# Expert weights fetched two parts to a transfer, fourteen small places, and the ranks of the experts made ahead of the first expert

## The chip, the cores and the metric

The kernel runs on one core of one Trainium2 chip. The metric is device time in microseconds. Several runs of the kernel before agree within 2.4 us, so about 0.2% is what a measurement of this kernel can tell from no change.

## The reference, cut to what matters

Two transformer blocks over 512 tokens of 1024 features, all in float32. The change lies in the second block's mixture of experts: 32 experts, 4 per token, each expert three 1024x1024 matrices (403 MB in all).

```python
def moe(xn, w_router, b_router, w_gate, b_gate, w_up, b_up, w_down, b_down):
    logits = (xt @ w_router).astype(jnp.float32) + b_router
    top_vals, top_idx = lax.top_k(logits, TOP_K)          # 4 of 32
    gates = jax.nn.softmax(top_vals, axis=-1)
    ...
        gt = jnp.minimum(xb @ w_gate[e] + b_gate[e], 7.0)
        up = jnp.clip(xb @ w_up[e] + b_up[e], -7.0, 7.0)
        hdn = (up + 1.0) * (gt * jax.nn.sigmoid(1.702 * gt))
        return hdn @ w_down[e] + b_down[e]
    ...
    out = jnp.zeros((N, D)).at[st].add(ybuf[dest] * sg[:, None])
```

## The kernel before, in words

**Float32 products** are made of two float32r halves: a weight tile `wraw` is cast to `whi` on ACT and the rest `wlo` is taken on DVE (`split`, L292); a product is three matmuls, hi·hi, hi·lo and lo·hi (`mm3`, L321 to L323).

**The expert stage** goes through `seq`: for each place p the 8 parts (128 rows of 1024) of gate, the 8 of up, and then the 8 of down of place p-1; 24 parts to a place, 768 in all. Places, not experts: a table `RANK` says which rank (by number of tokens) each place takes. Most places are big, with 112 rows (`CAP`): 6 matmuls of 512 columns to a part. The places in `FEW` are small, with 64 rows: there x_hi and x_lo stand side by side in one 128-wide operand, so that 4 matmuls do a part (L1684 to L1688); ahead of the next step ACT copies the lower half to `lower` and two matmuls fold it in (`hop`, `save_lower`, `fold_lower`). `FEW` has 12 places before. Tokens of an expert beyond its place's rows would go to a loop behind the stage (`overflow_rows`).

**Order of the work.** `fetch(i + 6)` ahead of part i splits parts 5 ahead of the product (`SPLIT_AHEAD`); `put(i, f)` hangs other work on part i (table `beside`), and `in_order` holds every engine but SP to the order in which the code is written. SP issues each weight transfer as soon as a buffer is free and the last transfer on the same of eight completion semaphores has landed. Raw tiles, `whi` and `wlo` share one ring of 4 KB slots that `Plan` hands out: 14 `s` slots, `x0`, `x1`, 15 `e` and 6 `y` slots.

**The start of the stage.** `choose`, `position` and `one_hot` find the tokens of expert 0; `gather(0)` fetches its rows on POOL's queue (L1494); `scale_rows` scales them, `turn_rows(0)` turns them on PE (L1654) and `split_rows(0)` splits them (`he`). Experts 0 and 1 have places 0 and 1 whatever their counts. From place 2 on a place needs the ranks: `ranks` (L1806, L1810) compares the 32 keys, `matches`, `places` and `places_end` (L1833 to L1849) make the row of each token's entry and scatter 16 tables, `picks` and `order_product` make `ranked`, which SP reads (`values_load`, L1528) ahead of the first weights of place 2. `third_place` (L1815 to L1822) finds the tokens of place 2. Before, all of it hangs on parts 0 to 13. The 16 tables come back on ACT's queue at parts 24 to 27 (`table_slots`, L1719), and `sum_tables` and `all_slots` make the slots of all other places of them.

Of the kernel before, what the change touches and what calls it, by code (L numbers as in the profile page):

```python
# [21 lines left out]
P = 128  # L22
# [12 lines left out]
FEW = [p for p in range(2, 30) if (p * 5) % 14 < 5] + [30, 31]  # L35
RANK = {p: p for p in (0, 1)}
RANK.update({p: 2 + i for i, p in enumerate(FEW)})
RANK.update({p: 2 + len(FEW) + i for i, p in enumerate(q for q in range(2, NE) if q not in FEW)})
# [26 lines left out]
def host_layout(i):  # L65
# [60 lines left out]
class Plan:  # L126
# [7 lines left out]
    def __init__(self, stages, slots, ahead, added=None, until=None, early=0):  # L134
# [8 lines left out]
        class State:  # L143
# [16 lines left out]
            def load(st):  # L160
                st.loads += 1
                return st.take(st.loads - 1)

            def split(st):
                i = st.splits
                ok = (st.loads > i or st.load()) and (kinds[i] == "r" or (st.take(i) and st.take(i)))
                if ok:
                    st.free.append(st.got[i][0])
                    st.splits += 1
                return ok  # L170

            def begin(st, u):

                i, k = first[u + 1], ahead(u)
                while i < n and k:
                    k -= kinds[i] == "p"
# [58 lines left out]
def build(tc, I, out, dbg=None, stop=None):  # L235
# [3 lines left out]
    with es:  # L239
# [558 lines left out]
        def attention(g, fill):  # L798
# [7 lines left out]
            for i in range(len(units) + AHEAD):  # L806
# [4 lines left out]
                if i in fill:  # L811
# [19 lines left out]
        open_ring("ring2", stages + ["p"] * (NE * 24), lambda u: 2 if u < experts - 1 else SPLIT_AHEAD if u >= experts else 0,  # L831
                  {forward - 1: [f"g{i}" for i in range(3)], mixer - 1: [f"p{i}" for i in range(5)], experts - 1: ['x0', 'e14', 'e13', 'e12', 'x1', 'e3', 'e4', 'e7', 'e8', 'e9', 'e10', 'e11', 'e5', 'e6', 'e0', 'e1', 'e2'], experts: ['y0', 'y1', 'y2', 'y3', 'y4', 'y5']}, {"g": mixer - 1, "p": mixer + 3}, mixer)
# [485 lines left out]
        for e in range(2):  # L1318
            nc.vector.tensor_scalar(out=keys[:, e:e + 1], in0=keys[:, e:e + 1], scalar1=100000.0 * (e - 2), scalar2=None, op0=ALU.add)
# [137 lines left out]
        more = [f"e{i}" for i in range(15)]  # L1457
# [5 lines left out]
        pick0 = early.tile([P, 2, 2], F32R, name="pick0")  # L1463
# [12 lines left out]
        for q in range(2):  # L1476
            nc.vector.tensor_copy(pick0[64 * q:64 * q + 64, q], eye[64 * q:64 * q + 64, 0:2])
# [44 lines left out]
        parts, expert = [], {0: 0, 1: 1}  # L1522

        def weights_of(n, p, k):
            rows = slice(k * P, (k + 1) * P)
            if p not in expert:
# [3 lines left out]
            return I["we_" + n][p, rows] if p < 2 else I["we_" + n][expert[p], rows, :].rearrange("o p n -> (o p) n")  # L1530
# [52 lines left out]
        weigh(1)  # L1583
        choose(0)
        position(0)
        one_hot(slot_of[:, :, 0:1], (0,), oh0)
        slot_products(ptok, oh0, (0,), 4, told)
        gi0 = tokens_of(ptok, 0)
# [5 lines left out]
        for tt in (1, 0):  # L1594
            store_normed(tt)
        weigh(0)
        pn = W["rb"][:, 2 * NT]
        for t2 in range(NT):
            nc.tensor.matmul(pn, ones, chosen[:, t2], start=t2 == 0, stop=t2 == NT - 1)
# [3 lines left out]
        nc.vector.scalar_tensor_tensor(out=keys, in0=pn, scalar=float(NE), in1=keys, op0=ALU.mult, op1=ALU.add)  # L1603
        nc.vector.tensor_copy(room, pn)
# [87 lines left out]
        def biased_product(ps, a, p, j):  # L1692

            def bias_of(start):
                t, r = (pick0, p) if p < 2 else (pick, RANK[p])
# [44 lines left out]
        psum, rows, pts = {}, {}, {}  # L1740
# [62 lines left out]

        def ranks():
            t = row_tile("cmp").rearrange("p (e f) -> p e f", f=NE)
            nc.vector.tensor_tensor(out=t, in0=keys[:, None, :].to_broadcast([P, NE, NE]), in1=keys[:, :, None].to_broadcast([P, NE, NE]), op=ALU.is_lt)  # L1806
            rows["cmp"] = t

        def ranks_end():
            nc.vector.reduce_sum(rank, rows.pop("cmp"), axis=AX)  # L1810

        def third_place():

            t = small.tile([P, NE], F32, tag="third", name="third", bufs=1)
            nc.vector.tensor_scalar(out=t, in0=rank, scalar1=float(RANK[2]), scalar2=None, op0=ALU.is_equal)  # L1815
            col = early.tile([P, NT, 1], F32, name="col2")
            u = row_tile("sel")[:, :NT * NE].rearrange("p (t e) -> p t e", e=NE)
            nc.vector.scalar_tensor_tensor(out=u, in0=slot_of, scalar=1.0, in1=t[:, None, :].to_broadcast([P, NT, NE]), op0=ALU.add, op1=ALU.mult)
            nc.vector.reduce_sum(col.rearrange("p t o -> p (t o)"), u, axis=AX)
            nc.vector.tensor_scalar(out=col, in0=col, scalar1=-1.0, scalar2=None, op0=ALU.add)  # L1820
            rows["oh2"] = new_one_hot()
            one_hot(col, range(NT), rows["oh2"])  # L1822

        def third_products():
            pts["tok2"] = ps_tr()
            slot_products(pts["tok2"], rows.pop("oh2"), range(NT), 2, [])

        def third_tokens():
            rows["gi2"] = tokens_of(pts.pop("tok2"), 2)

        def matches():
            t = rows["eq"] = row_tile("eqs")
            nc.vector.tensor_tensor(out=t[:, 0:512].rearrange("p (t k e) -> p t k e", k=4, e=NE), in0=iota[:, None, None, 0:NE].to_broadcast([P, NT, 4, NE]),  # L1833
                                    in1=choice[:, :, :, None].to_broadcast([P, NT, 4, NE]), op=ALU.is_equal)
            both = rows["both"] = row_tile("both")[:, :NT * NE].rearrange("p (t e) -> p t e", e=NE)
            nc.vector.scalar_tensor_tensor(out=both, in0=slot_of, scalar=float(NE), in1=rank[:, None, :].to_broadcast([P, NT, NE]), op0=ALU.mult, op1=ALU.add)

        def places():
            t = rows["eq"]
            v = [t[:, 512 * q:512 * q + 512].rearrange("p (t k e) -> p t k e", k=4, e=NE) for q in range(2)]  # L1840
            nc.vector.tensor_tensor(out=v[1], in0=v[0], in1=rows.pop("both")[:, :, None, :].to_broadcast([P, NT, 4, NE]), op=ALU.mult)

        def places_end():
            t = rows["eq"]
            at_ = small.tile([P, NT * 4], F32, tag="at", name="at", bufs=1)
            nc.vector.reduce_sum(at_, t[:, 512:D].rearrange("p (n e) -> p n e", e=NE), axis=AX)
            nc.vector.tensor_copy(place.rearrange("p t k -> p (t k)"), at_)
            for j, tb in enumerate(tables):
# [371 lines left out]
```

## Time and profile before

| | us |
|---|---|
| median of 3 runs | 2107.16 (2106.08 to 2108.41) |
| the profiled execution, its own time | 2103.72 |
| its span, first to last instruction | 2102.0 |
| PE busy | 1997.9 (95%) |
| DVE busy | 1647.1 (78%) |
| ACT busy | 1375.3 (65%) |
| weights of the experts | 768 transfers of 512 KB |

PE is TensorE's matmuls, DVE is VectorE, ACT ScalarE, POOL GpSimd, SP SyncE; ACTq and SPq are the queues on which these engines issue transfers. The granted clock is a share of TensorE's full 2.4 GHz. A matmul's record runs into the next one's, so sums of records are more than the time they cover; busy time counts each moment once.

### The profile page before, as it was taken

To read this page: it belongs to the slowest core of one execution; us is meant where nothing else is said; L and a number is where in the kernel's file an instruction comes from. 1 tells how busy PE (TensorE), PEld (TensorE's weight loads), DVE (VectorE), ACT (ScalarE), POOL (GpSimd) and SP (SyncE) were. 2 spreads that over 40 slices of the span, in tenths; PEclk is the share of its full clock that TensorE was granted. 3 is DMA by queue.
4 is the path that set the end of the run, shared out by engine and by line. 5 is a ranking of instruction groups with operands and counts; after the bars stand their busy time and mean duration, and the time that the engine had idled before them with its cause. 6 is when DMAs were issued, how large, how long until landed. Compare 5 with 4: busy or idle time off the path is not lost. (4 is left out here: it accounts for less than half of the span.)

```text
span 2102.0 us, 30256 instructions
## 1 busy us (share of the span) xinstructions
PE 1997.9 (95%) x9793; PEld 1537.2 (73%) x9794; DVE 1647.1 (78%) x2299; ACT 1375.3 (65%) x1883; POOL 463.5 (22%) x353
## 2 busy tenths in 40 slices
PE   8999999999999878878999999999999999999887
PEld 7777788888878877656677777767777777766565
DVE  6688873222476767577999999999999999999964
ACT  5656753222355455445788888888888888898831
POOL 0100110000010342214122323235232324153210
PEclk9999999999999999988999999999999999999999
DMA  5510554332565202567999999999999999999962
GB/s 212 170 31 22 194 207 161 100 96 94 200 214 180 90 31 101 216 205 262 349 400 383 404 394 400 402 398 403 397 395 401 384 396 396 384 401 388 368 240 80
DMA packets 168658, 554.29 MB, mean 264 GB/s; under 512 B 23075, under 2 KB 32291, under 8 KB 168492
## 3 DMA queue, kind: packets, MB, share of 16 engines
q1 hardware_dynamic: 145824, 510.06, 64.4%
q10 hardware_dynamic: 15116, 25.40, 3.5%
q0 software_dynamic: 7552, 16.82, 2.4%
q8 instruction: 79, 1.29, 0.2%
q14 instruction: 87, 0.71, 0.1%
HBM read 533.01 MB, written 27.05 MB: 266 GB/s over the span
## 5 line engine op out<-in xcount | busy, mean ns | idle before, releaser
L292 DVE TENSOR_TENSOR wlo<-wraw,whi 128x1024 fp32r<-128x1024 f32 x923 | 1080.7, 1216 | 224.7 <-ACT whi L292 220.7
L292 ACT CAST whi<-wraw 128x1024 fp32r<-128x1024 f32 x923 | 936.9, 1051 | 271.8 <-PE pw L323 126.4
L1666 POOL DMA_INDIRECT ybuf<-yt,si x31 | 247.8, 7994 | 428.7 <-ACT yt L1772 428.7
L322 PE MATMUL pw<-wlo,xe 128*112 128x512 f32 x608 | 239.9, 395 | 2.0 <-DVE wlo L292 2.0
L321 PE MATMUL pw<-whi,xe 128*112 128x512 f32 x608 | 241.2, 397 | 0.0
L323 PE MATMUL pw<-whi,xe 128*112 128x512 f32 x608 | 239.3, 394 | 0.0
L327 POOL TENSOR_SCALAR rstd<-ss 128x1 f32<-128x1 f32 (+1 forms) x68 | 25.1, 369 | 661.3 <-DVE ss L872 387.5
L321 PE MATMUL pw<-whi,he 128*112 128x512 f32 x352 | 142.5, 405 | 1.4 <-ACT whi L292 1.4
L1685 PE MATMUL pw<-wlo,xe 128*64 128x512 f32 x350 | 139.6, 399 | 3.9 <-DVE wlo L292 3.9
L1684 PE MATMUL pw<-whi,xe 128*128 128x512 f32 x350 | 139.4, 398 | 3.2 <-DVE xe L292 3.2
L322 PE MATMUL pw<-wlo,he 128*112 128x512 f32 x352 | 140.7, 400 | 1.7 <-DVE wlo L292 1.7
L323 PE MATMUL pw<-whi,he 128*112 128x512 f32 x352 | 140.3, 399 | 1.0 <-DVE he L292 1.0
L322 PEld LDWEIGHTS pw<-wlo,xe 128*112 128x112 f32 x608 | 106.0, 174 | 36.4 <-DVE wlo L292 2.8
L321 PEld LDWEIGHTS pw<-whi,xe 128*112 128x112 f32 x608 | 105.9, 174 | 35.1
L323 PEld LDWEIGHTS pw<-whi,xe 128*112 128x112 f32 x608 | 105.8, 174 | 35.0
L1494 POOL DMA_INDIRECT xg<-normed,gi x31 | 65.6, 2116 | 293.2 <-PE tr L1654 249.1
L1684 PEld LDWEIGHTS pw<-whi,xe 128*128 128x128 f32 x350 | 65.8, 188 | 31.4 <-DVE xe L292 3.6
L322 PEld LDWEIGHTS pw<-wlo,he 128*112 128x112 f32 x352 | 62.3, 177 | 23.7 <-DVE wlo L292 5.1
L321 PEld LDWEIGHTS pw<-whi,he 128*112 128x112 f32 x352 | 62.3, 177 | 22.5 <-ACT whi L292 2.2
L323 PEld LDWEIGHTS pw<-whi,he 128*112 128x112 f32 x352 | 62.2, 177 | 21.4 <-DVE he L292 1.4
L321 PE MATMUL pa<-x2T,whi 128*128 128x512 f32 (+1 forms) x200 | 72.6, 364 | 0.1
L322 PE MATMUL pa<-x2T,whi 128*128 128x512 f32 (+1 forms) x200 | 72.6, 363 | 0.0
(618 smaller groups left out, 4193.6 us busy)
## 6 DMA issues: line engine op xcount, KB each, us to landing
wraw<-in_we_gate_dram SPq DMA_DIRECT2D x256, 512.0 KB, 9.8
wraw<-in_we_up_dram SPq DMA_DIRECT2D x256, 512.0 KB, 9.6
wraw<-in_we_down_dram SPq DMA_DIRECT2D x256, 512.0 KB, 10.1
wraw<-in_w_gu_dram SPq DMA_DIRECT2D x44, 512.0 KB, 3.7
wraw<-in_w_down_dram SPq DMA_DIRECT2D x44, 512.0 KB, 3.7
wraw<-in_w_out_dram SPq DMA_DIRECT2D x24, 512.0 KB, 5.8
yb<-ybuf SPq DMA_DIRECT2D x6, 1024.0 KB, 9.8
wraw<-in_w_v_dram SPq DMA_DIRECT2D x10, 512.0 KB, 4.0
```

Source lines behind the costliest of these rows:

```text
L292: return nc.scalar.copy(hi, src), nc.vector.tensor_tensor(out=lo, in0=src, in1=hi.bitcast(F32), op=ALU.subtract)
L321: nc.tensor.matmul(o, a[0], b[0], start=start, stop=False)
L322: nc.tensor.matmul(o, a[0], b[1], start=False, stop=False)
L323: W["mm"] = nc.tensor.matmul(o, a[1], b[0], start=False, stop=stop)
L327: ins = nc.gpsimd.tensor_scalar(out=r[:, :w], in0=ss, scalar1=1.0 / n, scalar2=eps, op0=ALU.mult, op1=ALU.add)
L1494: nc.gpsimd.indirect_dma_start(out=xg[:m], out_offset=None, in_=src, in_offset=bass.IndirectOffsetOnAxis(ap=ap, axis=0), bounds_check=S - ...
L1666: nc.gpsimd.indirect_dma_start(out=ybuf, out_offset=bass.IndirectOffsetOnAxis(ap=ap, axis=0), in_=y_, in_offset=None, bounds_check=4 * S - ...
L1684: nc.tensor.matmul(ps[:, cs], a[:, k, 0:P], hi, start=first, stop=False)
L1685: nc.tensor.matmul(ps[:m, cs], a[:, k, 0:m], lo, start=False, stop=False)
```

## The change

- The experts' weights are laid out two parts to a row (`rows2` in `host_layout`), so that one transfer brings two parts, 1 MB with 8 KB for each partition, into one of ten buffers of their own (`units`: seven `E`, three `y`). `whi` and `wlo` keep the `s` slots, `x0`, `x1` and `e0`.
- `FEW` has 14 places, every second place for the most part: 3, 5, 7, 9, 12, 14, 16, 18, 21, 23, 25, 27, 30, 31 (before 3, 6, 9, 12, 14, 17, 20, 23, 26, 28, 30, 31).
- Expert 2 has a place of its own too (`STATIC = 3`), so that ranks are first needed at place 3, and `third_place` becomes one comparison.
- `matches`, `ranks` and `places` run on DVE between the issue of `gather(0)` and the scaling of its rows; five tables are scattered ahead of `gather(1)`, eleven behind it; `picks`, `gates_by_expert`, `gates_end` and `rooms` hang on later parts, spread out.

```diff
-FEW = [p for p in range(2, 30) if (p * 5) % 14 < 5] + [30, 31]
-RANK = {p: p for p in (0, 1)}
+STATIC = 3
+FEW = [3 + i * 9 // 4 for i in range(12)] + [30, 31]
+RANK = {p: p for p in range(STATIC)}
...
-        o["we_" + n] = i["w_" + n + "_2"][0]
+        o["we_" + n] = np.stack([rows2(w) for w in i["w_" + n + "_2"][0]])
...
+        units = ["E6", "E1", "E3", "E4", "E5", "E2", "E0", "y0", "y1", "y2"]
...
         def fetch(upto):
             while len(parts) < min(upto, len(seq)):
-                parts.append(load_part(weights_of(*seq[len(parts)])))
+                i = len(parts)
+                if i % 2 == 0:
+                    u = units[i // 2 % len(units)]
+                    W["pair"] = W[u if u in W else u[0]].tile([P, 2 * D], F32, tag=u, name="wraw", bufs=1)
+                    nc.sync.dma_start(W["pair"], weights_of(*seq[i]))
+                hi, lo = [slot_tile(t, F32R, n) for t, n in zip(W["plan"].next()[1:], ("whi", "wlo"))]
+                split(W["pair"][:, i % 2 * D:(i % 2 + 1) * D], hi, lo)
+                parts.append((hi, lo))
...
         weigh(1)
+        store_normed(1)
+        matches((1, 2, 3))
         choose(0)
...
         gather(0, base, CAP, gi0)
...
-        for tt in (1, 0):
-            store_normed(tt)
         weigh(0)
...
+        matches((0,))
+        ranks()
+        places()
...
-        fetch(1)
+        fetch(2)
         for cs in (slice(0, 512), slice(512, D)):
             scale_rows(xg[:CAP, cs], xg[:CAP, cs], norm0[:, 3:4], gpre[:CAP, cs])
+        store_normed(0)
...
-        put(0, gather, 1, normed, CAP, gi1)
-        for i, f in enumerate((ranks, ranks_end, third_place, matches, places, places_end, picks, gates_by_expert, gates_end)):
-            put(i, f)
-        put(6 + SPLIT_AHEAD + 1, order_product)
-        put(2 + SPLIT_AHEAD + 1, third_products)
-        put(2 + SPLIT_AHEAD + 2, third_tokens)
+        put(3, third_one_hot)
+        put(5, third_products)
+        put(6, third_tokens)
+        put(8, picks)
+        put(14, gates_by_expert)
+        put(8 + SPLIT_AHEAD + 1, order_product)
+        for tt in range(NT):
+            put(16 + 2 * tt, gates_end, tt)
...
-        put(15, rooms)
+        put(begin[1] + 5, rooms)
...
-        fetch(4)
+        scatter_entries(range(15, 10, -1))
         keep_warm(10, bias[:, 0:P], bias[:, 0:512])
         turn_rows(0)
         split_rows(0)
+        gather(1, normed, CAP, gi1)
+        scatter_entries(range(10, -1, -1))
```

DVE, from the scaling of the second norm of expert 0's rows (`norm`) to the first expert's first parts, before (`cmp` and `rank` are the ranks, `eqs`, `both`, `at` and `place` the places, `xg` the fetched rows):

```order
L1593 TENSOR_TENSOR norm_9021<-norm_9021 112x1
L347 SCALAR_TENSOR_TENSOR hx<-hx,rstd,g_ffn_norm_8599 128x1024 x2
...
L292 TENSOR_TENSOR wlo<-wraw,whi 128x1024
L347 SCALAR_TENSOR_TENSOR xg<-xg,norm_9021,g_ffn_norm_8599 112x512 x2
L292 TENSOR_TENSOR wlo<-wraw,whi 128x1024 x3
L292 TENSOR_TENSOR he<-tr,he 128x4x112 x2
L292 TENSOR_TENSOR wlo<-wraw,whi 128x1024 x2
L1806 TENSOR_TENSOR cmp<-keys 128x1024
L292 TENSOR_TENSOR wlo<-wraw,whi 128x1024
L1810 TENSOR_REDUCE rank<-cmp 128x32
```

and the same stretch now:

```order
L1643 TENSOR_TENSOR norm_9009<-norm_9009 112x1
...
L1563 TENSOR_TENSOR cmp<-keys 128x1024
L1564 TENSOR_REDUCE rank<-cmp 128x32
L1569 SCALAR_TENSOR_TENSOR both<-slot_of,rank 128x128
L1571 TENSOR_TENSOR eqs<-eqs,both 128x512
L1573 TENSOR_REDUCE at<-eqs 128x16
L1574 CAST place<-at 128x16
...
L297 TENSOR_TENSOR wlo<-wraw,whi 128x1024 x2
L352 SCALAR_TENSOR_TENSOR xg<-xg,norm_9009,g_ffn_norm_8600 112x512 x2
L352 SCALAR_TENSOR_TENSOR hx<-hx,rstd,g_ffn_norm_8600 128x1024
L297 TENSOR_TENSOR he<-tr,he 128x4x112 x2
L297 TENSOR_TENSOR wlo<-wraw,whi 128x1024 x7
```

The ranks and places moved from between the first splits to ahead of `xg`; of the two `hx` that stood there one went further ahead, one behind `xg`.

SP's queue where it first reads a rank (`ranked`), before:

```order
L303 DMA wraw<-in_we_up_dram 128x1024 x8
L303 DMA wraw<-in_we_down_dram 128x1024 x8
L1528 TENSOR_LOAD ranked
L303 ISA
L303 DMA wraw<-in_we_gate_dram 128x1024
```

and now:

```order
L1545 DMA wraw<-in_we_gate_dram 128x2048 x4
L1545 DMA wraw<-in_we_up_dram 128x2048 x4
L1545 DMA wraw<-in_we_down_dram 128x2048 x4
L1535 TENSOR_LOAD ranked
L1545 ISA
L1545 DMA wraw<-in_we_gate_dram 128x2048
```

The read moved behind the 24 parts of place 2; it stood behind part 39 and stands behind part 63.

## Rows read from the trace of the kernel before

**Rows 1.** The page: busy share of the DMA engines in 40 slices, tenths.

```profile
DMA  5510554332565202567999999999999999999962
```

**Rows 2.** Waits, 1050 to 1900 us: engine, line, waited for, us, times, longest.

```profile
ACT whi L292 <- PE pw L323: 89.4, 210, 1.2
DVE wlo L292 <- ACT whi L292: 24.3, 77, 1.0
...
ACT whi L292 <- DMA wraw<-in_we_gate_dram: 2.3, 2, 1.2
```

**Rows 3.** Groups by form, 1100 to 1900 us: count, busy us, mean ns, idle before.

```profile
L292 DVE TENSOR_TENSOR wlo<-wraw,whi 128x1024 fp32r<-128x1024 f32 x587 | 681.7, 1215 | 23.8 <-ACT whi L292 22.6 <-DMA wraw<-in_we_up_dram 0.7
...
L321 PE MATMUL pw<-whi,xe 128*112 128x512 f32 x489 | 193.9, 397 | 0.0
```

**Rows 4.** DMA queues, 1100 to 1900 us: packets, MB, share of 16 engines.

```profile
q1 hardware_dynamic: 83266, 303.18, 96.7%
```

**Rows 5.** Windows, places 12 to 16: busy PE, PEld, DVE, ACT, POOL; clock, DMA, GB/s.

```profile
1343.30:1372.10 28.80, 28.80 (x133) 20.39 (x132) 28.33 (x28) 27.78 (x32) 5.59 (x2) 1.00 1.02 396
1372.10:1405.40 33.30, 33.30 (x154) 24.21 (x153) 32.25 (x32) 27.77 (x32) 14.80 (x2) 1.00 1.03 409
1405.40:1436.70 31.30, 30.48 (x136) 20.09 (x135) 31.30 (x30) 29.97 (x33) 21.20 (x2) 1.00 1.01 404
1436.70:1468.90 32.20, 32.20 (x149) 23.79 (x148) 30.84 (x31) 26.34 (x29) 11.05 (x3) 1.00 1.03 399
1468.90:1506.20 37.30, 37.30 (x171) 27.88 (x170) 35.65 (x35) 30.69 (x34) 8.96 (x2) 1.00 1.02 395
```

**Rows 6.** Timeline of PE: the gate's bias at places 0, 3 and 30.

```profile
927.60 0.69 PE L1697 MATMUL pw<-bias,pick 128*112 128x512 f32 x2
...
1046.34 0.62 PE L1697 MATMUL pw<-bias,pick 128*64 128x512 f32 x2
...
1927.93 0.62 PE L1697 MATMUL pw<-bias,pick 128*64 128x512 f32 x2
```

**Rows 7.** Timeline of DVE, 932 to 950 us: four of the 21 instructions between splits.

```profile
932.43 1.21 DVE L1806 TENSOR_TENSOR cmp<-keys 128x1024 f32<-128x1024 f32 x1
...
934.70 1.21 DVE L1810 TENSOR_REDUCE rank<-cmp 128x32 f32<-128x1024 f32 x1
...
941.64 0.68 DVE L1841 TENSOR_TENSOR eqs<-eqs,both 128x512 f32<-128x512 f32 x1
...
949.20 1.18 DVE L1876 TENSOR_REDUCE gate_of<-eqs 128x32 f32<-128x128 f32 x4
```

**Rows 8.** Timeline of PE, 951 to 954 us, with the idle time before.

```profile
951.84 1.01 PE L1654 MATMUL tr<-ident,xg 112*128 112x112 f32 x4 [7.12 <-DVE gi L1502]
...
953.07 0.63 PE L322 MATMUL pw<-wlo,he 128*112 128x512 f32 x1
```

**Rows 9.** Timeline of DVE while expert 0's rows are fetched.

```profile
916.30 2.47 DVE L347 SCALAR_TENSOR_TENSOR hx<-hx,rstd,g_ffn_norm 128x1024 f32<-128x1024 f32 x2
...
924.36 1.41 DVE L347 SCALAR_TENSOR_TENSOR xg<-xg,norm,g_ffn_norm 112x512 f32<-112x512 f32 x2 [1.26 <-DMA xg<-base,gi]
```

**Rows 10.** Timeline of ACT, 974 to 996 us: the casts behind table loads.

```profile
984.50 1.05 ACT L292 CAST whi<-wraw 128x1024 fp32r<-128x1024 f32 x1 [5.52 <-DMA tabs<-table]
...
992.83 3.89 ACT L292 CAST whi<-wraw 128x1024 fp32r<-128x1024 f32 x4 [3.52 <-PE tr L1654]
```

**Rows 11.** SP's queue: a wait, and the issues of gate's parts of places 3 and 30.

```profile
SPq L1528 <- DVE ranked L1866: 10.7, 1, 10.7
...
1005.84 12.39 SPq L303 DMA_DIRECT2D wraw<-in_we_gate_dram  x8
...
1905.53 10.06 SPq L303 DMA_DIRECT2D wraw<-in_we_gate_dram  x8
```

**Rows 12.** The page, whole run: DMA queue, packets, MB, share of 16 engines.

```profile
q1 hardware_dynamic: 145824, 510.06, 64.4%
q10 hardware_dynamic: 15116, 25.40, 3.5%
```

More of the change, by code (lines that the diff above doesn't have):

```diff
@@ L1456, in build @@
         early = alloc("early")
-        more = [f"e{i}" for i in range(15)]
+        more = ["e0"] + [f"E{i}" for i in range(7)]
         for t in more:
@@ L1521, in build @@
         seq += [("down", NE - 1, k) for k in range(8)]
-        parts, expert = [], {0: 0, 1: 1}
+        parts, expert = [], {}
+        units = ["E6", "E1", "E3", "E4", "E5", "E2", "E0", "y0", "y1", "y2"]
         def weights_of(n, p, k):
-            rows = slice(k * P, (k + 1) * P)
-            if p not in expert:
+            if p >= STATIC and p not in expert:
                 r = RANK[p]
@@ new lines, in build, with matches @@
+        psum, rows, pts = {}, {}, {}
+        def matches(tiles):
+            if "eq" not in rows:
+                rows["eq"] = row_tile("eqs")
+            n = len(tiles)
+            t = slice(tiles[0], tiles[0] + n)
+            nc.vector.tensor_tensor(out=rows["eq"][:, 0:512].rearrange("p (t k e) -> p t k e", k=4, e=NE)[:, t], in0=iota[:, None, None, 0:NE].to_broadcast([P, n, 4, NE]),
+                                    in1=choice[:, t, :, None].to_broadcast([P, n, 4, NE]), op=ALU.is_equal)
@@ new lines, in ranks, with places @@
+        def ranks():
+            t = row_tile("cmp").rearrange("p (e f) -> p e f", f=NE)
+            nc.vector.tensor_tensor(out=t, in0=keys[:, None, :].to_broadcast([P, NE, NE]), in1=keys[:, :, None].to_broadcast([P, NE, NE]), op=ALU.is_lt)
+            nc.vector.reduce_sum(rank, t, axis=AX)
+        def places():
+            t = rows["eq"]
+            both = row_tile("both")[:, :NT * NE].rearrange("p (t e) -> p t e", e=NE)
+            nc.vector.scalar_tensor_tensor(out=both, in0=slot_of, scalar=float(NE), in1=rank[:, None, :].to_broadcast([P, NT, NE]), op0=ALU.mult, op1=ALU.add)
+            v = [t[:, 512 * q:512 * q + 512].rearrange("p (t k e) -> p t k e", k=4, e=NE) for q in range(2)]
+            nc.vector.tensor_tensor(out=v[1], in0=v[0], in1=both[:, :, None, :].to_broadcast([P, NT, 4, NE]), op=ALU.mult)
+            at_ = small.tile([P, NT * 4], F32, tag="at", name="at", bufs=1)
+            nc.vector.reduce_sum(at_, t[:, 512:D].rearrange("p (n e) -> p n e", e=NE), axis=AX)
+            nc.vector.tensor_copy(place.rearrange("p t k -> p (t k)"), at_)
@@ L1537, in build, with scatter_entries @@
+        def scatter_entries(js):
+            for j in js:
+                nc.gpsimd.indirect_dma_start(out=tables[j], out_offset=bass.IndirectOffsetOnAxis(ap=place[:, j // 4, j % 4:j % 4 + 1], axis=0), in_=entry[:, j // 4, j % 4], in_offset=None,
+                                             bounds_check=P * NE - 1, oob_is_err=False)
         traced = nc.cur_bb.bb.instructions
@@ L1587, in build @@
         slot_products(ptok, oh0, (0,), 4, told)
+        pn = W["rb"][:, 2 * NT]
+        for t2 in range(NT):
+            nc.tensor.matmul(pn, ones, chosen[:, t2], start=t2 == 0, stop=t2 == NT - 1)
         gi0 = tokens_of(ptok, 0)
@@ L1593, in build @@
         nc.vector.tensor_tensor(out=norm0[:, 3:4], in0=norm0[:, 1:2], in1=norm0[:, 2:3], op=ALU.add)
-        for tt in (1, 0):
-            store_normed(tt)
         weigh(0)
-        pn = W["rb"][:, 2 * NT]
-        for t2 in range(NT):
-            nc.tensor.matmul(pn, ones, chosen[:, t2], start=t2 == 0, stop=t2 == NT - 1)
+        nc.vector.scalar_tensor_tensor(out=keys, in0=pn, scalar=float(NE), in1=keys, op0=ALU.mult, op1=ALU.add)
+        nc.vector.tensor_copy(room, pn)
+        matches((0,))
+        ranks()
+        places()
         oh1, ptok1 = new_one_hot(), ps_tr(1)
@@ L1801, in last_rows @@
             return hi, lo
[L1804 to L1848, printed above, removed]
-                nc.gpsimd.indirect_dma_start(out=tb, out_offset=bass.IndirectOffsetOnAxis(ap=place[:, j // 4, j % 4:j % 4 + 1], axis=0), in_=entry[:, j // 4, j % 4], in_offset=None,
-                                             bounds_check=P * NE - 1, oob_is_err=False)
```

53 lines of the change are left out of this document (30 added, 23 removed).

## The prediction

> **What bounds the kernel now.** I read the 40 slices first: the DMA engines are busy nine tenths and more from the middle of the span to its end [rows 1], which is the expert stage, so the question is whether its 403 MB or an engine sets the pace. The waits of the stage answer it [rows 2]: ACT, which starts every split, waits 89.4 us for matmuls to give back a `whi` buffer, and 2.3 us for gate's weights; a transfer is hardly ever what comes last. The groups then give prices [rows 3]: 587 splits in 800 us, 1215 ns a record on DVE, which sits idle 23.8 us in all. A part is thus 1.36 us, of DVE's time nearly the whole. The windows cut that by place [rows 5], and here the reader should look longest:
>
> - a small place behind two big ones takes 28.80 us, all of them PE's;
> - a big place behind a small one takes 33.30 or 32.20, PE busy throughout, DVE 32.25 or 30.84;
> - a small place behind a single big one takes 31.30, and now DVE has every one of them and PE 30.48;
> - a big place behind a big one takes 37.30, PE throughout.
>
> So PE bounds the big places and DVE the small ones, and five parts split ahead carry some of DVE's time from a big place into the next small one. A pair small-big costs 28.80+33.30=62.1 when two big ones stood ahead of it and 31.30+33.30=64.6 otherwise.
>
> The transfers run alongside at nearly the same pace: 303.18 MB on the weights' queue in 800 us are 578 parts, 1.383 us each [rows 4], a little slower than the splits. They live on a lead, which shrinks: gate of place 3 is issued 40.5 us ahead of its first bias matmul, gate of place 30 22.4 us [rows 6, 11].
>
> The stage's start is its worst piece. From place 0's first bias matmul to place 3's go 118.7 us for 64 parts [rows 6]; at the big-behind-big price of rows 5 they are 16/24 x 37.3 + 2 x 37.3 = 99.5. So 19.2 us are lost there.
>
> **The change part by part.** The sum is made against the profiled execution, 2103.72 us for a span of 2102.0; it stands 3.4 us below the median, 2107.16, and I carry the difference over unchanged. About 0.2%, 4.2 us, is what a measurement of this kernel can tell from no change.
>
> *Ranks and places moved ahead.* Before, 21 instructions from `cmp` to the last `gate_of` stand between the splits [rows 7]; with DVE behind, the tokens of place 2 (L1502) come late, the turning of expert 1's rows holds a PSUM tile's turn, and PE idles 7.12 us [rows 8]. Then its clock is at half: matmuls take 0.63 instead of 0.40 us [rows 3, 8] for about 5 us (12 of them), 2.4 us lost if each takes 0.2 us longer. I take both away: -9.5. Cover: DVE has 8.06 us between the two rows of rows 9, while POOL's gather is under way. It loses 2.47 us of `hx` there and gains `cmp` and `rank`, 1.21 each, two places instructions of about 0.68 and a second split, some 1.2: 2.5 us more than before against a wait of 1.26 [rows 7, 9]. So expert 0's rows are scaled 1.2 to 1.5 us late: +1.5. If the fetch were shorter, all 2.5 would show. What stays between splits, the `oh`, `picks` and gate sums, is under half of the 21 and spread over 23 parts. Behind DVE's longer queue wait the splits of parts 2 and 3 and then PE; that is the 1.5 already counted.
>
> *POOL's queue.* Five scatters now stand ahead of `gather(1)` and eleven behind it. The gather waits for the last stored rows anyway, is needed ten parts (some 14 us) after the first matmul, and takes about as long as the first, 8 us [rows 9]: nothing. The tables end sooner, by about as much as the places do.
>
> *Table loads on ACT.* They share eight completion semaphores with the weights, and ACT stood 5.52 and 3.52 us before casts behind them [rows 10]; PE lost perhaps 5.5 of that. The tables are ready sooner, but the semaphores' earlier users are now 1 MB transfers. Bounds: -5.5 if all goes, +10 if each wait doubles. I take 0, for the wait shown is for a weight landing, whose bytes under way the buffers limit as before.
>
> *The rest of the 19.2.* 19.2-9.5-5.5=4.2 us I can't place; the bounds are all and none; half of it, -2.1, for part of it is buffers that refill after the two stalls.
>
> *SP's read of the ranks* moves from behind part 39 to behind part 63. It cost the weights' queue 10.7 us [rows 11], which ate from the lead and made nobody wait: nothing, but the lead is longer.
>
> *Fourteen small places.* Places 3 to 29 take 1927.93-1046.34=881.6 us [rows 6]. Now they are three times the same nine: s b s b s b s b b. By rows 5: 28.8+33.3, twice 31.3+33.3, 31.3+32.2, 37.3 = 292.1, times three 876.3: -5.3. Two places save 8 us each in PE's time, but DVE takes most of it: in a steady alternation it is the one that is full. Bounds: all pairs at 64.6, 12x64.6+3x37.3=887, +5.5; at DVE's own busy time, 31.30+32.25 a pair and 35.65 for a lone big one, 869.6, -12.
>
> *8 KB rows and 1 MB transfers.* Hardly any wait is for a landing [rows 2], so a faster queue gives nothing here; it lengthens a lead that is not used up. It can only count against the rival below.
>
> Sum: -9.5+1.5-2.1-5.3=-15.4. Profile 2088.3; median **2092 us**.
>
> **The rivals.**
>
> *PE's saving comes through* (lower). DVE loses part of its 21 instructions to the fetch and the split of two places' operands gets smaller; if the five parts ahead smooth better than in the one alternation the trace has (places 12 to 15), pairs come to DVE's own time, -12 for -5.3, and if the table wait and the unplaced 4.2 go too, -5.5 and -2.1 more: 2092-6.7-7.6=2078. For it: DVE idle 23.8 us in 800. Against: rows 5 show the alternation at 31.30.
>
> *The table loads wait longer* (near no change). Price +10, decided if their semaphores' earlier users are freshly issued 1 MB transfers: 2102.
>
> *The weights come too late* (slower). Ten buffers come back only when both halves are split, at the first matmul 14 parts can have landed (the `y` buffers are still other work's), and 754 are left. Place 30's gate, part 712, must land by 1927.9-15-7 (five parts ahead), 978 us after 927.6, so 698 parts at 1.40 us. The queue now does 1.383. If gaps between transfers make it 1% slower it binds; 3.4% slower (1.43) costs 21 us and turns the gain into +4 and more: at 5%, 2092+33=2125. For it: the margin is 1%. Against: a longer piece should be cheaper. From the whole-run queues [rows 12], time for a packet is 148 ns at 3498 B on q1 and 78 at 1680 on q10, so about 13 ns fixed and 0.039 ns a byte; an 8 KB piece would save 13 of 343 ns, 3.7%, an estimate. The Trainium skill, DMA: Bandwidth & Descriptors, section "Why small descriptors are slow (HBM only)", speaks against that gain: a packet's fixed cost is about 3 cycles and joining pieces pays only up to 256 B; by its figures, 128+3 cycles for 4 KB, the gain would be about 1%, an estimate, and the queue's pace 1.37. By either the sum is the same and this rival only gets rarer; no row here has rows of 8 KB.
>
> *The change doesn't do what it says*: two more small places would fail if the 14th smallest of the 29 counts were over 64; then the loop behind the stage fetches a whole expert again, 24 parts of 1.383 us, 33 us and more. Counting the reference's own choices for its default inputs gives 60 (and 88 for expert 2): 1 in 100.
>
> **How the numbers follow.** Forecast 0.57, its own range 2084 to 2101; PE's saving 0.20; table loads 0.13; weights late 0.08; the rest 0.02. Range for 8 in 10: 2073 to 2105, which leaves out the late weights and the best end of the second case. Faster by over 0.2% is below 2102.9: nearly all of the first two and half of the third, 0.81. Within: 0.10. Slower: the late weights and the loop, 0.09.
>
> **What would show it.** Right: no idle of several us on PE at expert 1's turning, and the clock full there; place 3 begins about 108 us after place 0; small places 31 us and big ones 33 in the alternating stretch, with DVE without idle; 384 weight transfers, and no ACT cast waiting for one. Wrong: pairs well under 64 us (DVE was not the limit), casts that wait for weights in the second half of the stage (the lead gone), longer idle of ACT behind the table loads, or any matmul of the loop behind the stage.

## The result, and the profile after

| | before | after |
|---|---|---|
| median of the runs, us | 2107.78 (2106.08 to 2109.28, 4 runs) | 2090.86 (2088.38 to 2091.52, 4 runs) |
| ratio, 95% interval | | 0.9915 (0.9899 to 0.993) |
| profiled execution: own time, span | 2103.72, 2102.0 | 2090.61, 2088.9 |

The changed kernel is 0.85% faster. Its gate's bias matmuls date the stage; PE's timeline after at places 0, 3, 30 and 31 (start, duration, line):

```profile
928.19 0.69 PE L1746 MATMUL pw<-bias,pick 128*112 128x512 f32 x2
...
1031.94 0.62 PE L1746 MATMUL pw<-bias,pick 128*64 128x512 f32 x2
...
1909.15 0.62 PE L1746 MATMUL pw<-bias,pick 128*64 128x512 f32 x2
...
1939.01 0.63 PE L1746 MATMUL pw<-bias,pick 128*64 128x512 f32 x2
```

Before, [rows 6] have places 0, 3 and 30, and this row place 31:

```profile
1960.22 0.63 PE L1697 MATMUL pw<-bias,pick 128*64 128x512 f32 x2
```

Against these the 13.1 us between the two spans fall apart so:

| stretch | before | after | difference |
|---|---|---|---|
| to place 0 | 927.60 | 928.19 | +0.6 |
| place 0 to 3 | 118.7 | 103.75 | -15.0 |
| place 3 to 30 | 881.6 | 877.2 | -4.4 |
| place 30 | 32.3 | 29.9 | -2.4 |
| place 31 to the end | 141.8 | 149.9 | +8.1 |

By this table alone the forecast's terms look roughly right: -11.6 at the start, -5.3 from place 3 to 30. One execution does not fix such stretches, though: a run below that has the same code up to the tail (48 idle matmuls) took 106.7 us from place 0 to 3 and 875.1 from 3 to 30. The waits of the stage, 1050 to 1900 us, say that something else happened; they answer to [rows 2]:

```profile
ACT whi L297 <- DMA wraw<-in_we_gate_dram: 34.3, 32, 3.0
...
DVE wlo L297 <- ACT whi L297: 22.7, 44, 1.0
ACT whi L297 <- DMA wraw<-in_we_down_dram: 17.6, 32, 1.4
ACT whi L297 <- PE pw L327: 10.5, 25, 1.4
...
ACT whi L297 <- DMA wraw<-in_we_up_dram: 7.6, 12, 1.6
```

The longest row of ACT's waits for matmuls has gone from 89.4 to 10.5 us, and in its place stand 34.3 + 17.6 + 7.6 = 59.5 us for weights. The windows of places 12 to 17 show where that begins (columns as in [rows 5]; small and big in turn):

```profile
1317.60:1346.10 28.50, 28.50 (x134) 20.61 (x133) 26.92 (x26) 26.02 (x30) 2.64 (x2) 1.00 1.01 400
1346.10:1379.30 33.20, 33.20 (x153) 24.16 (x152) 32.30 (x32) 28.05 (x32) 8.96 (x2) 1.00 1.02 406
1379.30:1408.40 29.10, 29.10 (x136) 20.73 (x135) 27.49 (x27) 26.64 (x30) 5.76 (x2) 1.00 1.01 396
1408.40:1441.60 33.20, 33.20 (x153) 24.16 (x152) 33.03 (x33) 27.76 (x32) 9.04 (x2) 1.00 1.02 408
1441.60:1475.00 33.40, 31.12 (x136) 20.01 (x135) 30.28 (x29) 29.29 (x34) 3.50 (x2) 1.00 1.00 389
1475.00:1508.20 33.20, 33.20 (x154) 24.15 (x153) 33.09 (x32) 27.63 (x32) 9.92 (x2) 1.00 1.01 406
```

The small place 14 behind a single big one takes 29.1 us, all PE's, where such a place took 31.30 of DVE's before. Place 16 is the same work and takes 33.4, with PE at 31.12 and DVE at 30.28: no engine fills it, and ACT stands 3.9 us there for gate's weights. The DMA engines' share is 1.00, but it is as high in the other windows; the run with fewer bytes below shows that they are what binds. A pair costs 62.3 us first and 66.6 then. The groups and the queue, 1100 to 1900 us, answer to [rows 3, 4]:

```profile
L297 DVE TENSOR_TENSOR wlo<-wraw,whi 128x1024 fp32r<-128x1024 f32 x591 | 683.1, 1213 | 24.8 <-ACT whi L297 22.7
...
L326 PE MATMUL pw<-whi,xe 128*112 128x512 f32 x448 | 177.9, 397 | 0.0
```

```profile
q1 hardware_dynamic: 42355, 308.46, 96.2%
...
wraw<-in_we_gate_dram SPq DMA_DIRECT2D x98, 1024.0 KB, 21.5
```

308.46 MB are 588 parts, 1.360 us each against 1.383. A transfer, now twice as long, lands 21.5 us after its issue (10.0 before). The gate of places 3 and 30 is issued here (SP's queue):

```profile
1002.40 8.21 SPq L1545 DMA_DIRECT2D wraw<-in_we_gate_dram  x4
...
1880.12 8.24 SPq L1545 DMA_DIRECT2D wraw<-in_we_gate_dram  x4
```

That is 29 us ahead of the bias at both places, against 40.5 and 22.4 [rows 6, 11]; around place 3 gate's transfers land in 7.8 us, so a lead is left there. Less the 21.5 to landing, 7.5 us are left at place 30, and five parts split ahead are 6.8: the lead is used up. On the page the DMA row has its nines to the end as before [rows 1]:

```profile
DMA  5510564222565302449999999999999999999762
```

At the start, PE's product for place 2's tokens and its turning of expert 1's rows, and then the DVE instructions that moved:

```profile
938.69 0.88 PE L1495 MATMUL tr<-info,oh 128*112 128x2 f32 x4 [2.83 <-DVE oh L1488]
949.54 0.93 PE L1703 MATMUL tr<-ident,xg 112*128 112x112 f32 x8
```

```profile
916.95 1.22 DVE L1564 TENSOR_REDUCE rank<-cmp 128x32 f32<-128x1024 f32 x1
...
919.98 0.17 DVE L1574 CAST place<-at 128x16 int32<-128x16 f32 x1
...
924.34 1.40 DVE L352 SCALAR_TENSOR_TENSOR xg<-xg,norm,g_ffn_norm 112x512 f32<-112x512 f32 x2
```

The turning does not wait any more (7.12 us before, [rows 8]); 2.83 us of wait are left, for the tokens of place 2, and the granted clock is at 0.50 behind them, from 938.4 to 945.2 us. In two runs below that have the same instructions up to place 3 (48 idle matmuls, twelve small places) the turning does wait, 4.6 and 3.3 us, for POOL's gather of expert 1's rows.

`xg` begins at 924.34 where it began at 924.36 [rows 9], but for another reason. Its rows were asked for at 915.10 and had landed at 919.55, after 4.45 us; before, at 916.43 and 924.34, after 7.91. So `xg` no longer waits for the fetch: it stands behind DVE's own work, which ranks and places make 4.5 us longer.

### The profile page after: what moved, and what is told of

It is laid out like the page before. It is cut to its first block, busy times and chain, and to the rows that moved or that the text cites. A ratio compares the mean times of both kernels' runs of the same rounds, so it can differ in the third digit from the quotient of the medians.

```text
span 2088.9 us, 28738 instructions
## 1 busy us (share of the span) xinstructions
PE 1986.1 (95%) x9709; PEld 1518.5 (73%) x9710; DVE 1642.1 (79%) x2297; ACT 1370.8 (66%) x1889; POOL 428.6 (21%) x353
## 5 line engine op out<-in xcount | busy, mean ns | idle before, releaser
L1715 POOL DMA_INDIRECT ybuf<-yt,si x31 | 217.7, 7022 | 447.7 <-ACT yt L1820 439.9
L326 PE MATMUL pw<-whi,xe 128*112 128x512 f32 x544 | 215.9, 397 | 0.0
L327 PE MATMUL pw<-wlo,xe 128*112 128x512 f32 x544 | 214.5, 394 | 0.5 <-DVE wlo L297 0.5
L328 PE MATMUL pw<-whi,xe 128*112 128x512 f32 x544 | 214.0, 393 | 0.0
L1734 PE MATMUL pw<-wlo,xe 128*64 128x512 f32 x406 | 164.0, 404 | 9.1 <-DVE wlo L297 8.7
L1733 PE MATMUL pw<-whi,xe 128*128 128x512 f32 x406 | 162.0, 399 | 3.2 <-DVE xe L297 3.2
L326 PE MATMUL pw<-whi,he 128*112 128x512 f32 x320 | 128.8, 403 | 0.0
L328 PE MATMUL pw<-whi,he 128*112 128x512 f32 x320 | 126.9, 396 | 0.0
L328 PEld LDWEIGHTS pw<-whi,xe 128*112 128x112 f32 x544 | 94.7, 174 | 31.4
L326 PEld LDWEIGHTS pw<-whi,xe 128*112 128x112 f32 x544 | 94.7, 174 | 31.2
L1733 PEld LDWEIGHTS pw<-whi,xe 128*128 128x128 f32 x406 | 76.8, 189 | 34.3 <-DVE xe L297 3.6
L1734 PEld LDWEIGHTS pw<-wlo,xe 128*64 128x64 f32 x406 | 54.7, 135 | 47.8 <-DVE wlo L297 32.4
L1733 PE MATMUL pw<-whi,he 128*128 128x512 f32 x182 | 73.2, 402 | 0.0
L328 PE MATMUL pa<-x2T,wlo 128*128 128x512 f32 (+1 forms) x200 | 72.6, 363 | 0.0
```

The source lines that it names most:

```text
L326: nc.tensor.matmul(o, a[0], b[0], start=start, stop=False)
L327: nc.tensor.matmul(o, a[0], b[1], start=False, stop=False)
L328: W["mm"] = nc.tensor.matmul(o, a[1], b[0], start=False, stop=stop)
L1715: nc.gpsimd.indirect_dma_start(out=ybuf, out_offset=bass.IndirectOffsetOnAxis(ap=ap, axis=0), in_=y_, in_offset=None, bounds_check=4 * S - ...
L1733: nc.tensor.matmul(ps[:, cs], a[:, k, 0:P], hi, start=first, stop=False)
L1734: nc.tensor.matmul(ps[:m, cs], a[:, k, 0:m], lo, start=False, stop=False)
```

## The experiments

Two theories. **A**: the weights' queue sets the end of the changed kernel, and the longer rows made the gain. **B**: PE and DVE set it, by the forecast's sum. Each ratio is to the kernel before on the same chip; the changed kernel's own is 0.9915. The 0.2% given at the top for the noise came of three runs: the fifteen of the kernel before beside the first experiments go from 2104.99 to 2112.67 us, 0.36%, so a ratio is read with its interval.

**Fewer bytes.** Every eighth transfer of weights from part 64 on is left out (44 of 384; the expectation's 88 are parts); the parts fetched before it are split and multiplied again.

```diff
-                if i % 2 == 0:
+                if i % 2 == 0 and not (i >= 64 and i // 2 % 8 == 7):
```

> The changed kernel without every eighth weight transfer from part 64 on (the two parts before are split and multiplied again in its place; 88 of 384 MB-transfers at most are left out, about 12 per cent of the bytes, no instruction of PE, DVE or ACT). Theory A: pairs of places stay at 62 us to the end, places 3 to 30 take 12 x 62.1 + 3 x 37.3 = 857 us instead of 877, and the last place's weights are there: 2062 to 2071. Theory B (DVE or PE sets 66 us for a late pair): 2086 to 2092, pairs still 64 to 67 us in the second half.

Measured 2063.22 us, ratio 0.9796 (0.978 to 0.9813). Places 3 to 30 take 854.7 us (857 expected). Windows of places 16 and 17, where the changed kernel took 33.4 and 33.2, and the one wait over 2 us of the casts that start the splits (`whi`):

```profile
1440.60:1469.60 29.00, 29.00 (x135) 20.87 (x134) 29.00 (x29) 28.80 (x33) 20.29 (x2) 1.00 0.93 357
1469.60:1502.80 33.20, 33.20 (x153) 24.16 (x152) 33.20 (x34) 27.91 (x32) 14.03 (x3) 1.00 0.98 382
```

```profile
ACT whi L297 <- PE pw L327: 22.9, 68, 0.3
```

No cast waits for weights. The same instructions on PE, DVE and ACT take 62.2 us a pair once the transfers are fewer. The queue holds the changed kernel, by some 25 us (0.9915 against 0.9796).

**Two transfers of 512 KB for one of 1 MB**, in the same buffers.

```diff
-                    nc.sync.dma_start(W["pair"], weights_of(*seq[i]))
+                    w = weights_of(*seq[i])
+                    for c in range(2):
+                        nc.sync.dma_start(W["pair"][:, c * D:(c + 1) * D], w[:, c * D:(c + 1) * D])
```

> The changed kernel with each 1 MB transfer made as two of 512 KB with 4 KB for a partition, in the same buffers. Theory A: the queue is slower by 1.6 to 1.8 per cent (two packets of 166 ns for one of 326), which over some 700 parts of 1.37 us is 15 to 17 us; with the lead already used up by place 16 most of it shows: 2100 to 2109, and ACT waits for weights over 80 us. Theory B: nothing, 2089 to 2093. If the 1 MB transfers themselves cost (coarser return of buffers), this run is faster than the changed kernel.

**The same with the old layout**, so that each 512 KB lie in one piece.

```diff
-        o["we_" + n] = np.stack([rows2(w) for w in i["w_" + n + "_2"][0]])
+        o["we_" + n] = i["w_" + n + "_2"][0]
...
-                    nc.sync.dma_start(W["pair"], weights_of(*seq[i]))
+                    for c in range(2):
+                        nc.sync.dma_start(W["pair"][:, c * D:(c + 1) * D], weights_of(*seq[i + c]))
...
```

> The changed kernel with the weights laid out as before: each 1 MB buffer is filled by two transfers of 512 KB, each a whole part that lies in one piece in memory. Theory R (what the change gains is the length of the row): the queue goes as in the run with two half transfers, 2110 to 2118. Theory S (there the 4 KB pieces with gaps between them cost something of their own: 168.7 ns a packet there, 166.3 in the kernel before, 1.4 per cent): 10 to 14 us less than that run, 2099 to 2104.

Measured 2114.0 us, ratio 1.0037 (1.0018 to 1.0056), and 2115.26 us, 1.0025 (1.0012 to 1.0038). Gaps between the pieces cost nothing; theory S falls, R holds. Without the 1 MB transfers of 8 KB rows, the rest of the change is slower than the kernel before, and more than theory A gave (its 2100 to 2109 was too small). The queue's rows, 1100 to 1900 us, of the first and of the second (whose profiled execution, 2119.91 us, was its slowest):

```profile
q1 hardware_dynamic: 82038, 298.72, 96.7%
```

```profile
q1 hardware_dynamic: 81589, 297.11, 96.7%
```

At the same busy share and row length the kernel before moved 303.18 MB. So about 1.5 to 2% are lost by filling one buffer with two transfers; why is open, and no run tried it. The engines were as busy as before, which speaks against too few transfers under way. The kernel before, with one transfer to a buffer, does not have this loss, so the two runs show more than the rows alone are worth: by the paces, 1.383 against 1.360 us for some 700 parts, that is 16 us, an estimate. No run has short rows without the loss.

**Twelve small places** in the changed kernel.

```diff
-FEW = [3 + i * 9 // 4 for i in range(12)] + [30, 31]
+FEW = [3, 6, 9, 12, 14, 17, 20, 23, 26, 28, 30, 31]
```

> The changed kernel with the old twelve small places. Theory A (in the second half of the expert stage the weights' queue sets the pace, so the two extra small places save nothing there): about no change against the changed kernel's 2090.9, 2089 to 2096, places 3 to 30 take 878 to 884 us, and ACT waits under 20 us for weights (58 us in the changed kernel). Theory B (the engines set the pace, as the forecast said): 5.3 us more by the forecast's own term, up to 16 by PE's time for two big places instead of two small ones, 2096 to 2107, and ACT's wait for weights changes little.

Measured 2092.42 us, 0.9929 (0.9913 to 0.9946). Theory A's no change holds; places 3 to 30 took 872.5 us, 5.5 less than even A expected, behind a place 3 that began at 1036.0. ACT's waits for weights:

```profile
ACT whi L297 <- DMA wraw<-in_we_down_dram: 2.9, 4, 1.1
ACT whi L297 <- DMA wraw<-in_we_gate_dram: 2.8, 4, 1.2
```

With twelve, PE is the bound and the weights arrive in time; with fourteen PE has less to do, and the queue takes over at the same end. The two more small places are worth nothing that these runs can tell.

**Fourteen small places in the kernel before**, nothing else.

```diff
-FEW = [p for p in range(2, 30) if (p * 5) % 14 < 5] + [30, 31]
+FEW = [3 + i * 9 // 4 for i in range(12)] + [30, 31]
```

> The kernel before with the fourteen small places alone (4 KB rows, 512 KB transfers, the old start). Theory A (weights' queue): it had a lead of 40.5 us at place 3 and 22.4 at place 30 and spends the rest of it, so 0 to 5 us are gained and then ACT waits for weights, over 20 us in all (2.3 for gate's before): 2103 to 2108 against 2107.8. Theory B (engines): the forecast's term, 5.3 us less, to 12 less: 2096 to 2102, and ACT hardly waits for weights.

Measured 2105.76 us, 0.9988 (0.9978 to 0.9999): 2.5 us less by the ratio. Places 3 to 30 took 878.3 us (1048.48 to 1926.75), 3.3 less. From place 12 on the places take what the forecast has for them (28.8, 31.3, 33.3, 32.2, 37.3); what it missed is place 3, 30.8 us here and 30.7 in the kernel before, not 28.8. ACT waits 12.8 us for weights, between the two theories: the old lead nearly lasts.

**Six pairs of `whi` and `wlo` buffers** in turn instead of eight.

```diff
...
-                hi, lo = [slot_tile(t, F32R, n) for t, n in zip(W["plan"].next()[1:], ("whi", "wlo"))]
+                s = W["plan"].next()[1:]
+                slot_names.append(s if i < 6 else slot_names[i - 6])
+                hi, lo = [slot_tile(t, F32R, n) for t, n in zip(slot_names[i], ("whi", "wlo"))]
```

> The changed kernel with only six pairs of whi and wlo buffers in turn instead of eight. Theory (the early pairs of places fell from 64.6 to 62.1 us because two more pairs let ACT and DVE run further ahead of PE): a big and the small place behind it take 64 to 65 us in places 3 to 10 as in the kernel before, ACT waits over 60 us for matmuls (13.7 us in the changed kernel); the total moves by 0 to 4 us only, since the weights' queue sets the end: 2090 to 2096. Rival (the early pairs are faster for another reason, such as ranks off the stream or longer transfers): 62 us, total unchanged.

Measured 2095.44 us, 0.9934 (0.9917 to 0.9952). Windows of places 14 and 15, and ACT's longest wait in sum:

```profile
1394.90:1426.20 31.30, 30.48 (x135) 20.07 (x134) 31.30 (x30) 30.01 (x33) 21.15 (x2) 1.00 1.01 401
1426.20:1459.40 33.20, 33.20 (x153) 24.18 (x152) 31.83 (x32) 27.27 (x31) 11.21 (x3) 1.00 1.02 401
```

```profile
ACT whi L297 <- PE pw L328: 89.0, 197, 1.2
```

There is the kernel before again: 31.30, DVE full, and 89 us of waits for matmuls. No cast waits for weights. The theory of the run holds: the layout of the change left eight pairs, so ACT and DVE could run two parts further ahead of PE, and DVE stopped binding. This kernel has the forecast's places and no cast that waits for weights, and its ratio is only 0.19% above the changed kernel's: the two bounds lie that close.

**Ranks, places and scatters back between the first splits.**

```diff
-        matches((0,))
-        ranks()
-        places()
...
+        put(0, ranks)
+        put(1, matches, (0,))
+        put(2, places)
+        put(2, scatter_entries, range(16))
         put(3, third_one_hot)
...
-        scatter_entries(range(15, 10, -1))
...
-        scatter_entries(range(10, -1, -1))
```

> The changed kernel with the ranks, the places and the 16 scatters back between the first splits (parts 0 to 2). The forecast's term for them is 9.5 - 1.5 = 8.0 us, part of it owed to the search for place 2's tokens, which stays out here. If it holds: expert 1's turning waits 4 to 7 us again, place 3 starts 4 to 9 us later than 1031.9, and 3 to 8 us of it show at the end: 2094 to 2099. Rival (the end hangs on the weights' queue alone, and its buffers come back when the splits are done, whatever PE waits for): place 3 later, the end within 2 us, 2089 to 2093.

Measured 2090.96 us, 0.9914 (0.9896 to 0.9932): the end does not move, as the rival said. PE waits 7.17 us for place 2's tokens instead of 2.83, and place 3 begins 5.0 us later:

```profile
941.66 0.88 PE L1495 MATMUL tr<-info,oh 128*112 128x2 f32 x4 [7.17 <-DVE oh L1488]
```

```profile
1036.91 0.62 PE L1743 MATMUL pw<-bias,pick 128*64 128x512 f32 x2
```

Of the 5.0 us, 3.8 came ahead of all that was edited: expert 0's gather is issued at 918.88 here, at 915.10 in the changed kernel. Counted from that issue, `xg` begins after 4.63 us instead of 9.24, place 0 after 7.5 instead of 13.1, and place 3 after 118.0 instead of 116.8: what the move wins behind place 0 it nearly pays ahead of it. The two runs with the changed kernel's instructions up to place 3 reach it after 119.1 and 120.7 us, so the 1.2 us can't be told from nothing. Places 3 to 30 then take 874.4 us, 2.8 less, and the rest of the 5 us is gone by the end.

**Table loads on POOL's queue.**

```diff
-                nc.scalar.dma_start(sums[j // 8][:, j % 8], tables[j].rearrange("(s e) c -> s (e c)", e=NE))
+                nc.gpsimd.dma_start(sums[j // 8][:, j % 8], tables[j].rearrange("(s e) c -> s (e c)", e=NE))
```

> The changed kernel with the 16 table loads on POOL's queue, so that no weight transfer stands behind one of them on a shared semaphore (SP waits 17.3 us for them, 10.2 at one time, and the DMA engines go at 0.6 to 0.9 from 976 to 992 us). If the weights' queue sets the end, the 3.8 us of queue time lost there come back: 2085 to 2089. If the tables now come later (POOL makes each of the 16 transfers itself) and the slots of place 3 with them: 2092 and more, with PE waiting for the turning of place 3's rows.

Measured 2089.46 us, 0.9916 (0.9895 to 0.9937): no difference that shows. SP's 17.3 us behind the table loads are gone and the DMA engines' share from 976 to 984 us rose from 0.95 to 1.02, but from 992 to 1000 it fell from 0.96 to 0.69, where SP waits for buffers.

**Four parts to a row** (16 KB; `units` becomes four buffers of 2 MB and two of 1 MB).

```diff
...
+                k = i % 8
+                n = 4 if k == 0 or (k == 4 and i // 8 % 2 == 0) else 2 if k in (4, 6) and i // 8 % 2 else 0
...
+                    nc.sync.dma_start(W["pair"], weights_of(*seq[i])[:, k % 4 * D:(k % 4 + n) * D])
```

> The changed kernel with four parts to a row (16 KB) in four buffers of 2 MB and two of 1 MB: three quarters of the weights come in transfers of 2 MB, the rest as 8 KB pieces of the longer rows. Theory A (the queue's pace sets the end, and a packet has a fixed cost): two 4 KB packets take 333 ns and one of 8 KB 326 ns, 6.5 ns for the one that is saved; the next doubling saves half of that for each 8 KB, 1 per cent, of three quarters of the bytes: 0.75 per cent of some 960 us, 7 us less, 2081 to 2087 against the changed kernel's 2091. If 16 KB rows are sent as two packets of 8 KB, or a buffer that comes back only after four splits costs the queue more than that: 2090 to 2100, with more of ACT's wait for weights.

Measured 2091.67 us, 0.9911 (0.9895 to 0.9928): no change. The queue, 1100 to 1900 us:

```profile
q1 hardware_dynamic: 26404, 308.44, 95.4%
```

The same bytes take 95.4% instead of 96.2%, 0.8% less. That is theory A's number by a mixture: a packet of 16 KB takes 639 ns, 2.0% less a byte than the changed kernel's 326 for 8 KB, and the 8 KB pieces of the longer rows take 337, 3.4% more. The queue moved no more for it, and ACT waits 77.7 us for weights: SP waits 633.8 us for splits to free a buffer (164.1 in the changed kernel, 1100 to 1900 us), for a buffer comes back only after four of them.

**More parts split ahead**, added to two of the edits above (ranks between the splits, tables on POOL).

```diff
-        fetch(2)
+        fetch(6)
...
+        fetch(7)
         keep_warm(10, bias[:, 0:P], bias[:, 0:512])
```

> The changed kernel with the ranks back on parts 0 to 2 and the tables on POOL's queue (both moved the end by nothing alone), and in the time that this frees on DVE seven parts are split ahead of the first matmul instead of two, so that buffers come back and the weights' queue, which stands almost still from 912 to 934 us, starts again sooner. If every part landed early counts at the end: 4 to 6 parts more at 960 us, 5 to 8 us less, 2082 to 2086. If the buffers' number caps the lead later on (SP waits for buffers again from 984 to 1000 us): what is won is lost by 1020 us, where again some 65 parts have landed, and the end stays at 2088 to 2092.

Measured 2093.24 us, 0.9916 (0.99 to 0.9933), above both ranges. Counted by the queue's 8 KB packets, 64 to a part, 58.0 parts had been moved by 990 us against 53.8, and 72.4 by 1020 us against 74.7. But the cause is not the cap alone, for a wait that the run brought along stood between:

```profile
DVE tab L1771 <- DMA tabs<-table: 9.0, 2, 6.5
...
POOL tabs L1765 <- DMA xg<-normed,gi: 4.7, 1, 4.7
```

POOL made its table loads behind a gather, DVE stood 9.0 us for them and split nothing meanwhile. What an earlier start of the queue is worth stays open.

**The tail.** After the last expert all engines branch. PE's rows there, before and after (the second number is the duration):

```profile
2013.47 1.62 PE L371 MATMUL tr<-whi 128*128 128x512 f32 x6 [1.06 <-DVEq L2094]
2014.93 0.40 PE L2002 MATMUL pw<-bdown,gateT 128*128 128x512 f32 x1
2015.26 0.72 PE L2004 MATMUL pw<-y,oh 64*128 64x512 f32 x2
```

```profile
1997.18 2.90 PE L376 MATMUL tr<-whi 128*128 128x512 f32 x6 [4.32 <-DVEq L2107]
1999.88 0.63 PE L2015 MATMUL pw<-bdown,gateT 128*128 128x512 f32 x1
2000.43 1.22 PE L2017 MATMUL pw<-y,oh 64*128 64x512 f32 x2
```

DVE's branch takes 3.7 us (1.2 before), PE stands 4.32 us, and then works at half clock (granted 0.61 from 1999 to 2009 us). The other runs built on the changed kernel have the longer wait too, 2.4 to 4.6 us, except that with six pairs, where PE stood 2.6 us there, most of it for a cast of ACT's; the kernel before with fourteen places has 1.1. Two edits: 48 idle matmuls instead of 30, and that with the tables on POOL.

```diff
-        keep_warm(30, wpg[0][0][:, 0:P], wpg[0][0][:, 0:512], last)
+        keep_warm(48, wpg[0][0][:, 0:P], wpg[0][0][:, 0:512], last)
```

> The changed kernel with 48 idle matmuls instead of 30 behind the last expert. In the changed kernel PE stands 4.3 us for DVE's branch to the code behind the expert stage (1.1 us in the kernel before), then works at half clock, and the rest of the tail takes 91.5 us from there instead of 88.4. If that idle time is what lowers the clock: PE idle under 1 us there, clock at full from about 1997 us on, the rest 88 to 90 us, the total 2 to 3 us less, 2087.5 to 2089.5. If the clock falls for another reason, or the 18 matmuls are themselves in the way: 2090 to 2093.

> The longer idle matmuls and the table loads on POOL's queue together: if both small gains are real, 3 to 5 us under the changed kernel, 2086 to 2088 against 2091; if the loads' gain of 1.5 us was chance, as the longer idle matmuls alone.

Measured 2090.02 us, 0.9906 (0.989 to 0.9923), and 2087.44 us, 0.9896 (0.988 to 0.9913). In the first, PE's wait and products are:

```profile
1997.51 1.62 PE L376 MATMUL tr<-whi 128*128 128x512 f32 x6 [1.22 <-DVEq L2107]
1998.97 0.40 PE L2015 MATMUL pw<-bdown,gateT 128*128 128x512 f32 x1
```

The clock granted from 1999 to 2009 us is 0.99. The idle time was what lowered it there; from place 31 to the end it takes 148.0 us instead of 149.9. The total, expected at 2087.5 to 2089.5, does not tell the two kernels apart. The second, 146.3, has the lowest ratio of all kernels that do the whole work, but the intervals overlap.

## Why the prediction was right, point by point

The total, the sign and the range were right: forecast 2092, measured 2090.86. The sum's reasons mostly were not, and that it meets the total to 1 us is luck: without the tail's +8.1, which the sum does not have, the profiled execution would have taken 2082.5 us; the forecast for it was 2088.3. Two of the text's own signs of being wrong came: pairs well under 64 us in places 3 to 15, and casts that wait for weights from place 16 on.

- **8 KB rows and 1 MB transfers: 0.** This step failed. The runs without them are 1.1 to 1.2% slower (ratios 1.0025 and 1.0037 against 0.9915), 23 to 26 us, more than the whole gain; by the paces some 16 of that, an estimate, and the rest goes with the unexplained loss of two transfers to a buffer. The text took a transfer that is hardly ever waited for as a resource with room to spare, although it had the pace of the queue, 1.383 us a part, above that of the splits, 1.36.
- **Fourteen small places: -5.3.** In the kernel before, the prices of the places hold, but the term came out at about half: 2.5 us measured (0.2 to 4.6 by the interval), 3.3 in the trace, as place 3 takes 30.8 us there and not the 28.8 of the sum. In the changed kernel it is worth nothing that shows. With six pairs of buffers the places take the 31.3 and 33.2 of the forecast. With the eight that it has, a pair takes PE's 62.1, and then 66.6 by the queue; that places 3 to 30 came out 4.4 us shorter is what these two leave of each other.
- **Ranks and places moved ahead: -9.5.** In the profiled execution the turning's wait went as said, though not the half clock, and from place 0 to 3 it took 15.0 us less against 11.6 forecast. But the move makes little of that. From the issue of expert 0's gather, place 3 comes after 116.8 us, after 118.0 with ranks and places back between the splits, and after 129.9 in the kernel before. Some 12 us come of what else the start changed: place 2's expert is fixed, the rest is spread over more parts, the buffers are others. No run parts these; with six pairs of buffers it is 121.6, hardly above the 120.7 of a run with eight. At the end the move is worth 0 (0.9914 against 0.9915): place 3 can come 5 us later, and the queue ends at the same time.
- **Later scaling: +1.5.** From the gather's issue `xg` came 1.3 us later than before (9.24 against 7.93), as forecast, and the issue 1.3 us sooner. The reason was another: the text's condition, a shorter fetch, came true (4.45 us instead of 7.91), and then all of the 4.5 us of ranks and places show.
- **POOL's queue: nothing.** This held by 3 us: the gather of expert 1's rows landed at 946.4, and the turning began at 949.5. In the two runs where PE waited for it, POOL's instruction took 5.7 and 6.0 us instead of 1.6; why is open.
- **Table loads: 0**, and SP's read of the ranks: 0. Both fit; ACT's longest wait for a table before place 3 was 1.9 us.
- **The weights come too late** was the right rival, priced wrongly. It was to bind at 1.40 us a part, the lead of places that take 64.6 us a pair. The queue got better, 1.360, and bound all the same, because the places asked for 62.1/48 = 1.29. (Its own example, 5% slower, comes to 35 us by its working, not 33.)
- **The queue's gain from long rows** was estimated at 3.7% from the fixed cost of a packet. [Rows 4] and the row after give 0.967/303.18 against 0.962/308.46 of the engines' time a MB, 2.2% less. The Trainium skill, DMA: Bandwidth & Descriptors, section "Why small descriptors are slow (HBM only)", gives about 1% by its 3 cycles a packet, an estimate; the measurement lies between the two. The sum had the gain at nothing, and that was its error.
- **PE's saving comes through** happened in places 3 to 15 (62.1), by buffers and not by a shorter DVE stream.
- **Not in the sum**: the tail, +8.1 (longer branch, half clock, the last place's parts 1.7 us later), and place 30, -2.4.

## What to carry to other kernels

Two engines and a queue within a few per cent of each other are one bound: a saving on one of them ends at the next. Before costing an edit at nothing because a resource is not waited for, compare its pace with the pace that the other edits will ask of it. And a sum that agrees with the trace stretch by stretch has not been tested; take one part away and see whether the end moves.

## What the runs showed of the hardware

- Rows of 8 KB took 2.2% less of the DMA engines' time a MB than rows of 4 KB. A packet of 16 KB took 639 ns, 2.0% less a byte than the 326 of 8 KB, but 8 KB pieces of 16 KB rows took 337.
- POOL's gather of the same 112 rows took 7.9 us from issue to landing in the kernel before and 4.45 in the changed one; that of expert 1's rows took 10.2 in the changed kernel and 14.6 with twelve small places, with the same instructions ahead of it. Unexplained.
- The same 4 KB rows, two transfers into one buffer, moved 1.5 to 2% less in the same busy time than one transfer into each of two buffers (298.72 and 297.11 MB against 303.18). Unexplained.
- A branch of all engines took DVE 1.2 us in the kernel before and 3.7 in the changed one, by the same code ahead of it; in the runs built on the changed kernel 0.7 (six pairs), 1.2 (four parts to a row) and otherwise 2.9 to 3.7. The page shows loads on the instruction queues (q8, q14) in both; which instruction waits for which was not tried.
